# One expert stage: a fixed TensorE order with the side steps in one piece each, and six more weight buffers

## Chip, cores and metric

The kernel runs on one core of one Trainium2 chip. The metric is the time of one execution on the device in microseconds (us), the median of several runs.

## What is computed

The reference is two small transformer blocks in float32, one after the other, on 256 tokens of width 1024. The first has gated linear attention, a dense feed-forward layer, sliding-window attention and a mixture of experts (the stage that this change touches); the second has two layers of differential and forgetting attention on 16 + 256 tokens. The part that matters here:

```python
def moe_swiglu(h, router, w_gate, w_up, w_down):
    t = h.reshape(B * S, D)                          # 256 x 1024
    logits = (t @ router).astype(jnp.float32)        # 8 experts
    top_val, top_idx = lax.top_k(logits, TOP_K)      # 2 of 8
    top_w = jax.nn.softmax(top_val, axis=-1)
    combine = jnp.sum(jax.nn.one_hot(top_idx, N_EXPERTS) * top_w[..., None], axis=1)
    for e in range(N_EXPERTS):
        out = out + combine[:, e:e + 1] * swiglu(t, w_gate[e], w_up[e], w_down[e])
    return out

def swiglu(h, w_gate, w_up, w_down):                 # 1024 -> 2816 -> 1024
    return (jax.nn.silu(h @ w_gate) * (h @ w_up)) @ w_down
```

## The kernel before

**Weights as a stream.** All large weights lie in DRAM in the order of their use, cut into units of 128 x 2048 floats (1024 KB; the gate and up units of an expert's last third are 768 KB). `load` issues one DMA per unit on SP's queue, in the stream's order, each as soon as its buffer is free. In the expert stage the units go round nine buffers: six of the tag `raw` (RING = 6) and three large ones, `rawx` (BIGS = 3). Outside that stage every unit is first split into a high and a low half-precision part (`split_unit`, ScalarE writes `wh`, VectorE `wl`, two pieces of 128 x 1024 each, six buffers of either tag, AHEAD_SPLIT = 6); the experts multiply the raw floats, so these twelve buffers lie idle there.

**The expert stage** (`moe`). A router picks two experts per token; the tokens of an expert are gathered into 96 columns (a "heavy" expert: number 7 and the four fullest of the others) or 64 (a "light" one). An expert has 35 units: per third b of its hidden width eight units of gate and up (`expert_gu`, k = 0 to 7) and four units of down, three in the last third (`expert_down`). `moe_order` lists the 24 thirds of all experts: the gate and up units of one, then the down units of the one before it. A heavy unit is 12 matmuls in the program, a light one 8, on 32 columns of the array each, four side by side; a float32 matmul leaves two records in the trace. The light experts' thirds are strewn between the heavy ones'.

**Side steps.** Between the weight units TensorE also has, per third, the transposes of the hidden values (`hidden`: `eg` and `egb` in, `eh` out by VectorE); per pair of experts to come, four gathers (`chunks`: `G` with `tokH`, then `tokL`) and one step `back` (transposes of `Gb`, and sums with `wrr`); per finished expert, two scatters (`scatter`: `GT` with `yH` and `yL`, into one bank named `mm` for the upper half of the rows and one named `acc` for the lower, which VectorE adds to the residual `h`). `expert_gu` calls `between` after k = 3, which hands out one `hidden`, up to two scatters and up to three gathers. Where each single instruction of them then stands on TensorE is the scheduler's choice by its own estimate of times: only SP's order is written by hand (`manual_schedule` in `run`).

**Into the next stage.** The second block begins with weights that are split again: `split_ahead`, called with every raw unit, splits up to three of them (SPLIT_AHEAD) while the last seven expert units are used. `feed(u)` scales and squares two of the eight 128-row chunks of `h` for the next norm. A branch (`crowded`, L1170), taken only if an expert has too many tokens, stands before the first expert; SP and all others read its count there.

Of the kernel before, what the change touches and what calls it, by code (L numbers as in the profile page):

```python
# [11 lines left out]
F32 = mybir.dt.float32  # L12
# [14 lines left out]
UW = 2048  # L27
# [251 lines left out]
RING = 6  # L279
AHEAD_SPLIT = 6  # L280
BIGS = 3
WORK = 11
AHEAD = RING + BIGS
SPLIT_AHEAD = 3
# [6 lines left out]
class Build:  # L291
# [59 lines left out]
    def load(self, between=None):  # L351
        u = self.next_load
        self.next_load += 1
        i = u - self.moe_range[0] if u in self.moe_range else 0
        if i % (RING + BIGS) >= RING:
            r = self.big("rawx", (128, UW))
        else:
            r = self.ring.tile([128, UW], F32, name="raw", tag="raw", bufs=RING)
        kind, place, rank = self.uses[u]
        w = 4 * int(kind[2:]) if kind[:2] == "gu" else UW  # L360
        n = w // (2 if u < 2 else 1)
        if rank is None:
            src = self.aps["stream"][place]
        else:
            if self.at is None:
                self.at = [self.nc.values_load(self.places[0:1, j:j + 1], engines=[mybir.EngineType.SP],
                                               min_val=EXPERTS_AT, max_val=EXPERTS_AT + 6 * EXPERT_UNITS)
                           for j in range(7)]
            src = self.aps["stream"][bass.ds(self.at[rank] + place, 1)].rearrange("a p w -> (a p) w")
        for i in range(0, w, n):  # L370
            self.nc.sync.dma_start(r[:, i:i + n], src[:, i:i + n])
            if between is not None:
                between(i)
        self.loaded[u] = r

    def raw_unit(self, kind):
        u = self.next_unit
        self.next_unit += 1
        assert self.uses[u][0] == kind, (u, self.uses[u], kind)
        self.split_ahead(u)  # L380
        while u not in self.loaded:
            self.load()
        return self.loaded.pop(u)
# [8 lines left out]

    def split_ahead(self, u):
        n = len(self.halves)
        for v in range(u, min(u + 7, len(self.uses))):
            if v >= u + 1 and not u in self.moe_range:
                break
            if v in self.moe_range or v in self.halves or v < self.split_to:
                continue
            if n >= SPLIT_AHEAD:  # L400
                break
            while v not in self.loaded:
                self.load()
            self.halves[v] = self.split_unit(self.loaded.pop(v), self.uses[v][0])
            self.split_order.append(self.last_high)
            self.split_to, n = v + 1, n + 1

# [566 lines left out]
    def moe(self):  # L974
# [77 lines left out]
        self.prefetch()  # L1052
        self.crowded(cnti)
        late, last, ahead = [], None, []

        starts = dict(zip(HEAVY, GATHERED[1:]))
        for e, kind, b in moe_order():
            units = self.raw_units(e, kind, b)
            if kind == "gu":
# [3 lines left out]

                def between(last=last):
                    if last:
                        st[last] = self.hidden(st[last], last[1])
                    for queue, n in ((late, 2), (ahead, 3)):
                        for f in queue[:n]:
                            queue.remove(f)
                            f()  # L1070

                st[e, b] = self.expert_gu(st[e], b, units, between)
                last = (e, b)
                continue
            if (e, b) == (HEAVY[-1], 2):
                assert not ahead
                st[e, b] = self.hidden(st[e, b], b)
                while late:
                    late.pop(0)()
                self.next_norm("moe")  # L1080
            self.expert_down(st[e], b, st.pop((e, b)), units)
            if b == 2:
                late += self.expert_out(st.pop(e))
        for f in late:
            f()
        for m in range(4):
            self.feed(m)

# [59 lines left out]
    def raw_units(self, e, kind, b):  # L1148

        for u in moe_units(e, kind, b):  # L1150
            r = self.raw_unit(u[0])
            w = chunk(b)[1] if kind == "gu" else 512
            yield [r[:, j * w:(j + 1) * w] for j in range(4)]

# [10 lines left out]
    def crowded(self, cnti):  # L1165
# [4 lines left out]
        with self.tc.If(nc.values_load(cnti[0:1, 0:1], min_val=0, max_val=2 * S) > S, label="crowded"):  # L1170
            p1, pn = (self.t(n, [128, 2, 8], bufs=1) for n in ("pos1", "pos1n"))
            w1, wn = (self.t(n, [128, 2, 8, 2], bufs=1) for n in ("wr1", "wr1n"))
            for r in range(2):
                nc.vector.tensor_sub(p1, self.pos, self.slots[:, None, :].to_broadcast([128, 2, 8]))
                nc.vector.tensor_scalar(p1, p1, -96.0 * r, None, op0=OP.add)
                nc.vector.tensor_copy(w1, self.wr)
                with self.tc.For_i(0, E, 1) as e:
                    X = [self.wk("xg2", (128, 4, 96)) for _ in range(2)]
# [75 lines left out]
    def expert_gu(self, s, b, units, between=None, again=False):  # L1254
# [6 lines left out]
        for k, blk in enumerate(units):  # L1261
# [7 lines left out]
            if not s["light"]:  # L1269
                for j in range(4):  # L1270
                    self.mm1(ps[2][j * GROUP:(j + 1) * GROUP, :W], x[:, 64:96], blk[j], **go)
            if between is not None and k == 3:
                between()
        g = (self.wk if again else self.m2)("eg", [128, 512])
# [10 lines left out]
    def hidden(self, gs, b):  # L1285
# [3 lines left out]
        for g in gs:  # L1289
# [4 lines left out]
            for k in range(n):  # L1294
                self.nc.tensor.transpose(pt[:, k * m:(k + 1) * m], g[:, k * 128:(k + 1) * 128], self.ident[0:m, 0:m])  # L1295
            h = self.wk("eh", (128, 4, m))
            self.nc.vector.tensor_copy(h[:, :n], pt[:, :n * m].rearrange("p (k s) -> p k s", k=n))  # L1297
# [425 lines left out]
```

## Time and profile before

| | |
|---|---|
| median of 3 runs | 1488.23 us (1487.46 to 1488.7) |
| the profiled execution | 1489.77 us |
| its span, first to last instruction | 1488.0 us |
| TensorE busy | 1433.7 us (96%) |
| VectorE, ScalarE busy | 620.2 us, 506.8 us |
| mean granted TensorE clock | 0.985 |
| DMA | 386.90 MB, mean 260 GB/s |

The profile is of one execution. A group of instructions has a busy time, a mean duration and the idle time that stood before it with what ended it. TensorE's records overlap (a matmul begins before the one ahead of it has drained), so the time that a matmul costs is the distance from its start to the next start, not its duration; and a busy TensorE is not yet one at its peak.

### The profile page before, as it was taken

What the parts mean: (1) busy time and instruction counts of PE and PEld (TensorE: products, weight loads), DVE (VectorE), ACT (ScalarE), POOL (GpSimd) and SP (SyncE); (2) the same over time, 40 slices, a digit from 0 to 9 for tenths busy, and PEclk for the clock granted to TensorE, in tenths of its full rate; (3) what the DMA queues carried; (4) which work ended last, traced back from release to release, by engine and by line L of the source; (5) the groups of instructions that cost most, each with busy time, mean ns of one, the idle gap of its engine ahead of it and who ended that gap; (6) DMA issues with size and microseconds to landing.
All of it is one profiled execution on the core that took longest, in us unless ns stands there. A gap on an engine that the chain in (4) does not pass through costs nothing.

```text
span 1488.0 us, 29082 instructions
## 1 busy us (share of the span) xinstructions
PE 1433.7 (96%) x12306; PEld 947.1 (64%) x12306; DVE 620.2 (42%) x1260; ACT 506.8 (34%) x1015; POOL 47.9 (3%) x105
## 2 busy tenths in 40 slices
PE   7999999999979999999999999999998999999997
PEld 7999999998864433333433243333334988898987
DVE  6886555576731011101210020111006876677663
ACT  5766444466411000000100010000005765676563
POOL 1011000010000000000000000000002000010000
PEclk9999999999969999999999999999998999999999
DMA  9433555542408899999989999999998432243300
GB/s 353 163 153 142 192 182 194 189 154 111 175 7 328 321 421 383 381 398 420 419 355 419 421 352 420 419 421 420 419 418 337 142 140 92 92 161 142 114 2 29
DMA packets 58649, 386.90 MB, mean 260 GB/s; under 512 B 7408, under 2 KB 8816, under 8 KB 18448
## 3 DMA queue, kind: packets, MB, share of 16 engines
q1 hardware_dynamic: 58224, 383.64, 65.6%
q8 instruction: 98, 1.61, 0.4%
q0 software_dynamic: 288, 1.34, 0.2%
q14 instruction: 39, 0.32, 0.1%
HBM read 383.90 MB, written 1.05 MB: 259 GB/s over the span
## 4 chain that ended last, share of the span: by engine, by line
PE 62%; DVE 3%; DMA 2%; ACT 2%; issue 1%; DVEq 0%; ACTq 0%
PE mm L436 29%; PE acc L436 16%; PE mm L428 5%; PE mm L429 5%; PE mm L427 5%; DVE wl L433 1%; DMA rawx<-stream 1%; DMA raw<-stream 1%; ACT wh L432 1%; PE acc L1295 1%; PE mm L1295 1%; PE acc L1517 0%; DVE eg L1276 0%; PE acc L1440 0%; DVE h L1342 0%
## 5 line engine op out<-in xcount | busy, mean ns | idle before, releaser
L427 PE MATMUL mm<-xH,wh 128*128 128x256 f32 (+1 forms) x1072 | 309.8, 290 | 13.2 <-ACT wh L432 10.0
L429 PE MATMUL mm<-xH,wl 128*128 128x256 f32 (+1 forms) x1072 | 306.3, 286 | 0.7 <-DVE wl L433 0.7
L428 PE MATMUL mm<-xL,wh 128*128 128x256 f32 (+1 forms) x1072 | 306.2, 286 | 0.7 <-DVE xL L525 0.7
L433 DVE TENSOR_TENSOR wl<-raw,wh 128x1024 fp32r<-128x1024 f32 x198 | 242.0, 1229 | 108.0 <-ACT wh L432 107.7
L432 ACT ACTIVATE wh<-raw 128x1024 fp32r<-128x1024 f32 x198 | 207.2, 1057 | 179.5 <-PE mm L428 118.6
L427 PEld LDWEIGHTS mm<-xH,wh 128*128 128x128 f32 x1072 | 204.0, 191 | 15.9 <-ACT wh L432 10.0
L436 PE MATMUL mm<-raw,xg 128*32 128x512 f32 (+1 forms) x1944 | 209.4, 569 | 4.3 <-DVEq L1170 4.3
L428 PEld LDWEIGHTS mm<-xL,wh 128*128 128x128 f32 x1072 | 203.6, 190 | 2.0 <-DVE xL L525 1.4
L429 PEld LDWEIGHTS mm<-xH,wl 128*128 128x128 f32 x1072 | 203.5, 190 | 1.5 <-DVE wl L433 1.0
L478 ACT ACTIVATE eg<-mm,ws 128x512 f32<-128x512 f32 (+1 forms) x24 | 15.6, 652 | 429.3 <-PE mm L436 429.3
L436 PEld LDWEIGHTS mm<-raw,xg 128*32 128x32 f32 x1944 | 64.0, 111 | 122.2 <-issue 116.5
L436 PE MATMUL acc<-raw,eh 128*32 128x512 f32 x1248 | 141.6, 593 | 0.0
L1276 DVE SCALAR_TENSOR_TENSOR eg<-mm,ws,eg 128x512 f32<-128x512 f32 (+1 forms) x24 | 17.0, 706 | 254.6 <-PE mm L436 254.6
L436 PE MATMUL mm<-rawx,xg 128*32 128x512 f32 (+1 forms) x936 | 97.2, 555 | 0.0
L436 PEld LDWEIGHTS acc<-raw,eh 128*32 128x32 f32 x1248 | 40.1, 110 | 88.0 <-issue 85.9
L436 PE MATMUL mm<-raw,xl 128*32 128x512 f32 (+1 forms) x752 | 80.4, 560 | 0.4 <-DMA raw<-stream 0.4
L427 PE MATMUL mm<-oH,wh 128*128 128x256 f32 (+1 forms) x256 | 73.2, 288 | 0.1
L428 PE MATMUL mm<-oL,wh 128*128 128x256 f32 (+1 forms) x256 | 72.5, 284 | 0.1
L429 PE MATMUL mm<-oH,wl 128*128 128x256 f32 (+1 forms) x256 | 71.9, 281 | 0.0
L436 PE MATMUL acc<-rawx,eh 128*32 128x512 f32 x600 | 69.1, 593 | 0.1
L436 PEld LDWEIGHTS mm<-rawx,xg 128*32 128x32 f32 x936 | 29.8, 110 | 57.5 <-issue 54.6
L1297 DVE COPY eh<-mm 128x512 f32<-128x512 f32 (+3 forms) x19 | 10.2, 538 | 133.9 <-PE mm L1295 133.9
(411 smaller groups left out, 1907.6 us busy)
## 6 DMA issues: line engine op xcount, KB each, us to landing
raw<-stream SPq DMA_DIRECT2D x243, 1024.0 KB, 7.9
rawx<-stream SPq DMA_DIRECT2D x70, 1024.0 KB, 10.8
raw<-stream SPq DMA_DIRECT2D x41, 768.0 KB, 8.5
rawx<-stream SPq DMA_DIRECT2D x23, 768.0 KB, 8.3
raw<-stream SPq DMA_DIRECT2D x4, 512.0 KB, 8.7
h<-xT SPq DMA_DIRECT2D x4, 256.0 KB, 6.5
out<-y SPq DMA_DIRECT2D x4, 256.0 KB, 2.4
pc<-t_gla POOLq DMA_DIRECT2D x1, 384.0 KB, 5.3
```

The costliest lines, as they stand in the source:

```text
L427: mm(out, a[0], b[0], start=start, stop=False, skip_group_check=True)
L428: mm(out, a[0], b[1], start=False, stop=False, skip_group_check=True)
L429: mm(out, a[1], b[0], start=False, stop=stop, skip_group_check=True)
L432: self.last_high = self.nc.scalar.activation(h, src, AF.Copy).ins
L433: self.nc.vector.tensor_sub(l, src, h.bitcast(F32))
L436: self.last_mm = self.nc.tensor.matmul(out, a, b, start=start, stop=stop, skip_group_check=True).ins
L478: self.last_silu = self.nc.scalar.activation(out, src, AF.Silu, **kw).ins
L1276: nc.vector.scalar_tensor_tensor(g[:, :W], ps[1][:, :W], s["rsA"], g[:, :W], op0=OP.mult, op1=OP.mult)
L1295: self.nc.tensor.transpose(pt[:, k * m:(k + 1) * m], g[:, k * 128:(k + 1) * 128], self.ident[0:m, 0:m])
L1297: self.nc.vector.tensor_copy(h[:, :n], pt[:, :n * m].rearrange("p (k s) -> p k s", k=n))
```

## The change

TensorE's order in the expert stage is fixed: `rows_of_experts` is traced under `manual_schedule` for PE, so instructions stand there as the program writes them. `between` is called after every unit: after k = 1 it makes the transposes of the third before, after k = 3 and after k = 5 one whole scatter or gather step. Before the last three down units the scatters now come ahead of the transposes, and two units of the next block are split behind them; `feed` goes 0, 2, 1, 3. Fifteen units instead of nine are loaded ahead: after six `raw` and three `rawx`, six units go as two halves into a `wh` and a `wl` buffer, by two DMAs each; the last fifteen expert units go round the nine as before. The narrow `eh` takes another buffer tag.

```diff
@@ -280,7 +280,8 @@
 AHEAD_SPLIT = 6
 BIGS = 3
 WORK = 11
-AHEAD = RING + BIGS
+EXTRA = 6
+AHEAD = RING + BIGS + EXTRA
 SPLIT_AHEAD = 3
 SCATTER_FROM = 1
 EXPERTS_AT = next(i for i, p in enumerate(stream_plan(ALL)) if p[1].startswith("moe"))
@@ -351,14 +352,19 @@
     def load(self, between=None):
         u = self.next_load
         self.next_load += 1
+
         i = u - self.moe_range[0] if u in self.moe_range else 0
-        if i % (RING + BIGS) >= RING:
+        cycle = AHEAD if i + AHEAD < len(self.moe_range) else RING + BIGS
+        kind, place, rank = self.uses[u]
+        w = 4 * int(kind[2:]) if kind[:2] == "gu" else UW
+        n = w // (2 if u < 2 else 1)
+        if i % cycle >= RING + BIGS:
+            n = w // 2
+            r = [self.ring.tile([128, UW // 2], F32, name=t, tag=t, bufs=AHEAD_SPLIT)[:, :n] for t in ("wh", "wl")]
+        elif i % cycle >= RING:
             r = self.big("rawx", (128, UW))
         else:
             r = self.ring.tile([128, UW], F32, name="raw", tag="raw", bufs=RING)
-        kind, place, rank = self.uses[u]
-        w = 4 * int(kind[2:]) if kind[:2] == "gu" else UW
-        n = w // (2 if u < 2 else 1)
         if rank is None:
             src = self.aps["stream"][place]
         else:
@@ -368,7 +374,7 @@
                            for j in range(7)]
             src = self.aps["stream"][bass.ds(self.at[rank] + place, 1)].rearrange("a p w -> (a p) w")
         for i in range(0, w, n):
-            self.nc.sync.dma_start(r[:, i:i + n], src[:, i:i + n])
+            self.nc.sync.dma_start(r[i // n] if isinstance(r, list) else r[:, i:i + n], src[:, i:i + n])
             if between is not None:
                 between(i)
         self.loaded[u] = r
@@ -377,7 +383,6 @@
         u = self.next_unit
         self.next_unit += 1
         assert self.uses[u][0] == kind, (u, self.uses[u], kind)
-        self.split_ahead(u)
         while u not in self.loaded:
             self.load()
         return self.loaded.pop(u)
@@ -390,20 +395,13 @@
         self.next_unit += 1
         return self.halves.pop(u)
 
-    def split_ahead(self, u):
-        n = len(self.halves)
-        for v in range(u, min(u + 7, len(self.uses))):
-            if v >= u + 1 and not u in self.moe_range:
-                break
-            if v in self.moe_range or v in self.halves or v < self.split_to:
+    def split_ahead(self, u, n=1):
+        for v in range(u, u + n):
+            if v in self.halves:
                 continue
-            if n >= SPLIT_AHEAD:
-                break
             while v not in self.loaded:
                 self.load()
             self.halves[v] = self.split_unit(self.loaded.pop(v), self.uses[v][0])
-            self.split_order.append(self.last_high)
-            self.split_to, n = v + 1, n + 1
 
     def prefetch(self):
         while self.next_load < min(self.next_unit + AHEAD, self.moe_range[-1] + 1):
@@ -1051,7 +1049,15 @@
         steps[-1]()
         self.prefetch()
         self.crowded(cnti)
+        with self.tc.manual_schedule(engines={mybir.EngineType.PE}):
+            self.rows_of_experts(st, gather)
+        for i in (0, 2, 1, 3):
+            self.feed(i)
+
+    def rows_of_experts(self, st, gather):
+
         late, last, ahead = [], None, []
+        self.again = False
 
         starts = dict(zip(HEAVY, GATHERED[1:]))
         for e, kind, b in moe_order():
@@ -1061,30 +1067,29 @@
                     assert not ahead
                     ahead = gather(starts[e])
 
-                def between(last=last):
-                    if last:
+                def between(k, last=last):
+                    if k == 1 and last:
                         st[last] = self.hidden(st[last], last[1])
-                    for queue, n in ((late, 2), (ahead, 3)):
-                        for f in queue[:n]:
-                            queue.remove(f)
-                            f()
+                    elif k in (3, 5) and (late or ahead):
+                        (late or ahead).pop(0)()
 
                 st[e, b] = self.expert_gu(st[e], b, units, between)
                 last = (e, b)
                 continue
-            if (e, b) == (HEAVY[-1], 2):
+            final = (e, b) == (HEAVY[-1], 2)
+            if final:
                 assert not ahead
-                st[e, b] = self.hidden(st[e, b], b)
                 while late:
                     late.pop(0)()
+                st[e, b] = self.hidden(st[e, b], b)
                 self.next_norm("moe")
             self.expert_down(st[e], b, st.pop((e, b)), units)
             if b == 2:
                 late += self.expert_out(st.pop(e))
+            if final:
+                self.split_ahead(self.next_unit, 2)
         for f in late:
             f()
-        for m in range(4):
-            self.feed(m)
 
     def rank_experts(self, sel, cnti):
 
@@ -1150,7 +1155,10 @@
         for u in moe_units(e, kind, b):
             r = self.raw_unit(u[0])
             w = chunk(b)[1] if kind == "gu" else 512
-            yield [r[:, j * w:(j + 1) * w] for j in range(4)]
+            if isinstance(r, list):
+                yield [r[j // 2][:, (j % 2) * w:(j % 2 + 1) * w] for j in range(4)]
+            else:
+                yield [r[:, j * w:(j + 1) * w] for j in range(4)]
 
     def units_again(self, e, kind, b):
 
@@ -1174,6 +1182,7 @@
                 nc.vector.tensor_sub(p1, self.pos, self.slots[:, None, :].to_broadcast([128, 2, 8]))
                 nc.vector.tensor_scalar(p1, p1, -96.0 * r, None, op0=OP.add)
                 nc.vector.tensor_copy(w1, self.wr)
+                self.again = True
                 with self.tc.For_i(0, E, 1) as e:
                     X = [self.wk("xg2", (128, 4, 96)) for _ in range(2)]
                     xs = [[X[c // 2][:, 2 * (c % 2):2 * (c % 2) + 2] for c in range(4)]]
@@ -1269,8 +1278,8 @@
             if not s["light"]:
                 for j in range(4):
                     self.mm1(ps[2][j * GROUP:(j + 1) * GROUP, :W], x[:, 64:96], blk[j], **go)
-            if between is not None and k == 3:
-                between()
+            if between is not None:
+                between(k)
         g = (self.wk if again else self.m2)("eg", [128, 512])
         self.silu(g[:, :W], ps[0][:, :W], scale=s["rsA"])
         nc.vector.scalar_tensor_tensor(g[:, :W], ps[1][:, :W], s["rsA"], g[:, :W], op0=OP.mult, op1=OP.mult)
@@ -1293,7 +1302,7 @@
             pt = self.scratch()
             for k in range(n):
                 self.nc.tensor.transpose(pt[:, k * m:(k + 1) * m], g[:, k * 128:(k + 1) * 128], self.ident[0:m, 0:m])
-            h = self.wk("eh", (128, 4, m))
+            h = (self.wk if m == 128 or self.again else self.m1)("eh", (128, 4, m))
             self.nc.vector.tensor_copy(h[:, :n], pt[:, :n * m].rearrange("p (k s) -> p k s", k=n))
             out.append(h)
         return out
```

TensorE where expert 3 begins (its first gate and up units are `rawx,xg` and `raw,xg`) and expert 7's scatter is due (`GT`). Before:

```order
L436 MATMUL acc<-rawx,eh 32x512 x12
L436 MATMUL acc<-GT,yH 128x256
L436 MATMUL mm<-rawx,xg 32x512 x12
L436 MATMUL mm<-GT,yH 128x256
L436 MATMUL mm<-GT,yL 128x256
L436 MATMUL acc<-GT,yL 128x256
L436 MATMUL mm<-GT,yH 128x256
L436 MATMUL mm<-rawx,xg 32x512 x12
L436 MATMUL acc<-GT,yH 128x256
L436 MATMUL mm<-GT,yL 128x256
L436 MATMUL acc<-GT,yL 128x256
L436 MATMUL mm<-raw,xg 32x512 x12
```

The same place after; the row of transposes (`par,eg`) belongs to the light expert's third before.

```order
L1304 MATMUL acc<-par,eg 128x128 x4
L434 MATMUL mm<-raw,xg 32x512 x24
L434 MATMUL mm<-GT,yH 128x256
L434 MATMUL acc<-GT,yH 128x256
L434 MATMUL mm<-GT,yL 128x256
L434 MATMUL acc<-GT,yL 128x256
L434 MATMUL mm<-GT,yH 128x256
L434 MATMUL acc<-GT,yH 128x256
L434 MATMUL mm<-GT,yL 128x256
L434 MATMUL acc<-GT,yL 128x256
```

The scatter was strewn over single units, with `mm` and `acc` in changing turns; now a whole step of sixteen stands between two units, `mm` and `acc` strictly by turns, and the transposes stand two units into the next third, not at the end of their own.

VectorE before the last three down units, where `eh` is what those units read. Before:

```order
L1326 SCALAR_TENSOR_TENSOR yL<-acc,ws,yH 128x512
L1297 COPY eh<-mm 128x384
L1297 COPY eh<-acc 128x192
L1342 TENSOR_TENSOR h<-h,mm 128x2x256
L1342 TENSOR_TENSOR h<-h,acc 128x2x256
L1342 TENSOR_TENSOR h<-h,mm 128x2x256
L1342 TENSOR_TENSOR h<-h,acc 128x2x256
```

After:

```order
L1335 SCALAR_TENSOR_TENSOR yL<-acc,ws,yH 128x512
L1351 TENSOR_TENSOR h<-h,mm 128x2x256
L1351 TENSOR_TENSOR h<-h,acc 128x2x256
L1351 TENSOR_TENSOR h<-h,mm 128x2x256
L1351 TENSOR_TENSOR h<-h,acc 128x2x256
L1306 COPY eh<-mm 128x384
L1306 COPY eh<-acc 128x192
```

The two copies moved behind the four additions of the last light expert's scatter.

SP, after the loads of the stages before and the first nine expert units (the last rows `raw` and `rawx` here), up to the branch's count:

```order
L377 DMA rawx<-stream 128x2048 x3
L377 DMA wh<-stream 128x1024
L377 DMA wl<-stream 128x1024
L377 DMA wh<-stream 128x1024
L377 DMA wl<-stream 128x1024
L377 DMA wh<-stream 128x1024
L377 DMA wl<-stream 128x1024
```

Twelve loads of 512 KB (six of them shown) came in ahead of SP's read of `cnti`; before, that read followed the three `rawx`.

## Rows read from the trace of the kernel before

**Rows 1.** What SP's queue waited for: us in total, times, longest

```profile
SPq L371 <- PE mm L436: 361.0, 180, 14.3
SPq L371 <- PE acc L436: 152.9, 84, 5.4
```

**Rows 2.** Stretches: length; busy PE, PEld, DVE, ACT, POOL; granted clock, DMA share, GB/s

```profile
439.20:1132.30 693.10, 682.45 (x6393) 244.03 (x6393) 91.13 (x201) 58.63 (x124) 1.65 (x6) 0.99 0.97 393
900.00:920.00 20.00, 20.00 (x191) 6.06 (x183) 0.56 (x1) 0.00 (x0) 0.00 (x0) 1.00 1.01 421
10.00:15.00 5.00, 4.32 (x18) 4.03 (x19) 4.94 (x6) 4.51 (x10) 2.01 (x3) 1.00 1.07 347
862.50:865.00 2.50, 2.50 (x13) 0.61 (x17) 0.36 (x1) 0.33 (x1) 0.00 (x0) 0.50 1.01 420
1135.00:1140.00 5.00, 2.94 (x25) 2.45 (x26) 5.00 (x6) 4.35 (x6) 0.00 (x0) 0.66 0.97 380
```

**Rows 3.** Weight matmuls by group, 439.2 to 1132.4 us: first and last of six

```profile
L436 PE MATMUL mm<-raw,xg 128*32 128x512 f32 (+1 forms) x1944 | 209.4, 569 | 4.3 <-DVEq L1170 4.3
...
L436 PE MATMUL mm<-rawx,xl 128*32 128x512 f32 (+1 forms) x400 | 41.9, 555 | 0.0
```

**Rows 4.** Chain that ended last: start us, us, what

```profile
510.54 0.59 PE acc L1295 x4
511.12 0.39 PE mm L1295 x4
...
590.48 10.30 PE mm L436 x96
...
654.50 15.53 PE mm L436 x192
```

**Rows 5.** TensorE in time, 830 to 870 us: start, us, instruction, [idle before]

```profile
835.06 0.66 PE L1295 MATMUL acc<-par,eg 128*128 128x128 f32 x4 [0.94 <-DVE eg L1276]
...
843.40 2.76 PE L436 MATMUL mm<-rawx,xg 128*32 128x512 f32 x24
...
846.51 2.78 PE L436 MATMUL mm<-rawx,xg 128*32 128x512 f32 x24
...
856.09 0.28 PE L436 MATMUL acc<-GT,yL 64*128 64x256 f32 x1
856.21 0.27 PE L436 MATMUL acc<-GT,yH 64*128 64x256 f32 x1
```

**Rows 6.** TensorE in time, 438 to 470 us: one gather

```profile
454.38 0.68 PE L436 MATMUL mm<-G,tokH 128*128 128x160 f32 x4
...
455.43 5.36 PE L436 MATMUL mm<-raw,xg 128*32 128x512 f32 x48
```

**Rows 7.** TensorE in time, 596 to 606 us: the step `back`

```profile
603.28 0.44 PE L1236 MATMUL acc<-par,Gb 128*128 128x128 f32 x2 [0.35 <-DVE Gb L1206]
...
603.99 1.04 PE L436 MATMUL mm<-raw,xg 128*32 128x512 f32 x2
```

**Rows 8.** TensorE, then VectorE, at the stage's end

```profile
1122.35 0.50 PE L436 MATMUL mm<-GT,yH 64*128 64x256 f32 x2 [0.81 <-ACT yH L1325]
...
1123.36 0.28 PE L436 MATMUL acc<-GT,yL 64*128 64x256 f32 x1
1123.37 0.28 PE L436 MATMUL mm<-GT,yH 64*128 64x256 f32 x1
1123.48 0.28 PE L436 MATMUL acc<-GT,yH 64*128 64x256 f32 x1
...
1124.53 5.36 PE L436 MATMUL acc<-rawx,eh 128*32 128x512 f32 x48
...
1123.80 0.69 DVE L1342 TENSOR_TENSOR h<-h,mm 128x512 f32<-128x512 f32 x1
...
1143.21 5.67 DVE L525 SCALAR_TENSOR_TENSOR xL<-h,g,xH 128x256 fp32r<-128x256 f32 x8
```

**Rows 9.** DMA issues of the page: KB each, median us from issue to landing

```profile
raw<-stream SPq DMA_DIRECT2D x243, 1024.0 KB, 7.9
```

## The prediction, before the changed kernel was run

> **What bounds the kernel now.** I looked first for the engine that the expert stage waits for. The list of SP's waits says it: SP, which issues the weight loads, stood 361.0 + 152.9 = 513.9 us waiting for TensorE to free a buffer [rows 1]. A queue that waits for its consumer is not the bound. The table of stretches agrees: from 439.20 to 1132.30, which is the stage, TensorE is busy 682.45 of 693.10 us [rows 2]. The same row gives the DMA a busy share of 0.97, which would make it look like a second bound; its rate tells more: 393 GB/s over the stage against 421 in a stretch where it is pressed [rows 2], so there is about 7% in hand, not more. A gain on TensorE of much over 7% (some 45 us) would meet the stream.
>
> Busy TensorE is not TensorE at its peak, so the next question is what of the 693 us is weight work. A record costs the distance to the next start. The chain gives this cleanly, since it shows unbroken runs: 96 records in 10.30 us, 107.3 ns each, and in an expert's narrower last third 192 in 15.53 us, 80.9 ns each [rows 4]. A heavy unit leaves 24 records, a light one 16. Five heavy experts of 35 units and three light ones make 5 x 35 x 24 + 3 x 35 x 16 = 5880; the six groups of weight matmuls, 1944 the first and 400 the last, add up to the same [rows 3]. Narrow are the gate and up units of the last thirds, 5 x 8 x 24 + 3 x 8 x 16 = 1344. So 4536 x 107.3 ns + 1344 x 80.9 ns = 486.7 + 108.7 = 595 us. The remaining **98 us** are side steps, the breaks that they make, and waits. Only these can the change move: it touches no weight matmul.
>
> **A strewn step, read in time.** A unit with two pairs of `GT` matmuls strewn into it takes 846.51 - 843.40 = 3.11 us from its start to the next one's [rows 5]; 24 records alone take 24 x 107.3 ns = 2.575. The 0.535 us more are two pairs at 0.12 each (`mm` and `acc` started together, the next 0.12 later: 1123.36, 1123.37, 1123.48 [rows 8]) and about 0.295 for leaving the weight stream and coming back. Two successive `GT` matmuls into the same bank take 0.12 each instead: 856.09, 856.21 [rows 5]. Two of different banks share one slot. Transposes at 835.06 stood 0.94 us because `eg` had just been begun by VectorE [rows 5]; five light thirds of the trace show such a stand.
>
> **The change on TensorE, worked from below.** Each step after the change, priced by rows:
> - Transposes of the hidden values: a full heavy third 0.59 + 0.39 = 0.98 us for two groups of four [rows 4]. Ten of these, five heavy thirds with six transposes (0.74, scaled), six light with four (0.59), three light with three (0.44): 9.8 + 3.7 + 3.5 + 1.3 = 18.3.
> - Gathers: 455.43 - 454.38 = 1.05 us for one [rows 6]; sixteen in the stage: 16.8, as an upper price, for the light pairs are narrower.
> - `back`: 603.99 - 603.28 = 0.71 [rows 7]; eleven such groups in the stage: 7.8.
> - Scatters: all 208 `GT` matmuls now go by turns into `mm` and `acc`, 104 slots where the old order makes 151. Of the 104, 88 lie ahead of the stage's last three units and behind its start: 88 x 0.12 = 10.6.
> - Breaks: the steps stand in 56 pieces between units (68 before): 56 x 0.295 = 16.5.
> - The end: 3 (next paragraph but one). Waits that stay, at the start and at a step whose input is late: 4, an estimate by four stands like the 0.94 above.
>
> Sum: 18.3 + 16.8 + 7.8 + 10.6 + 16.5 + 3 + 4 = **77 us**, against 98. The gain is 21.
>
> **Worked from above,** by what goes: 47 slots of 0.12 = 5.6; twelve breaks = 3.5; five stands at `eg`, which had 0.94 to wait [rows 5] and now have two more units (at least 2 x 16 x 107.3 ns = 3.4 us) between the last gate unit and the transposes, = 4.7. A clock at 0.50 (1.2 GHz, the lower level) in 862.5 to 865 [rows 2], where TensorE did single `GT` matmuls between units, costs half of what runs in it, 1.25 us; if whole steps do not bring it down, that goes too. That makes 15, less 2.7 for the end, 12.3. The remaining 9 us by which the two ways differ would have to be gathers, strewn in chunks whose inputs ScalarE and VectorE were still making; I did not find one row for each. I take a figure near the first way, **20**, since its terms are durations of every step and the second is a list of the losses that I happened to find; 12 is kept as an end of the range.
>
> **The end of the stage.** Now the transposes and the `eh` copies come before the last scatters and the last three down units start at 1124.53 [rows 8]. Afterwards `eh` stands on VectorE behind four additions to `h`. The first began at 1123.80 and took 0.69 [rows 8], so four end at 1126.6 and two copies, taken at 0.3 each by their width against that addition, at 1127.2: 2.7 us later than 1124.53, TensorE idle meanwhile (3 with what the second scatter's wait for `yH`, 0.81 now [rows 8], leaves over). A stand there may also be followed by a lower clock: 0.66 in 1135 to 1140, where TensorE was busy 2.94 of 5 us [rows 2]. The last three units are 72 records, 7.7 us at the upper level and double at the lower, so this end costs 3 to 10.7. I take 3. In return the additions are done sooner, and the splitting of the next block's first two units and `feed` (`xL` starts at 1143.21 [rows 8]) have a shorter way; I cost the tail behind the last unit at 0, from -2 to +2, since the same operations of the same engines stand there in another order.
>
> **The six units ahead.** They do nothing by themselves while SP waits for TensorE. Their twelve DMAs stand on SP ahead of the branch's count, but `wh` and `wl` lie idle by then, so I cost that at nothing; if a buffer were still in use, the stage's start would wait for it, with a unit's 7.9 us from issue to landing [rows 9] as the bound. Their use is that TensorE, being faster, draws the stock down sooner. From the middle of the stage, where gathers give the stream its last long rest (about 846 us after the change), 101 units are left beyond fifteen full buffers, 76 of 1.049 MB and 25 of 0.786, 99.4 MB: at 421 GB/s [rows 2] 236 us, done near 1082. TensorE needs the last near 1106: 24 us in hand. With nine buffers 107 units, 251 us: near 1097, almost bound.
>
> The halves are the unknown. The upper bound is the rate now, 421 GB/s. The lower is the stretch 10 to 15 us, where DMAs of 512 KB and smaller moved 347 [rows 2]. Forty of the 101 units are halves; at 347 each costs 1.049 MB/347 - 1.049 MB/421 = 0.53 us more, 21 us in all, most of the reserve. I take 421, as the stretch of 347 is also the program's first loads with little queued.
>
> The page has loads of 1024 KB that need 7.9 us to land [rows 9] while, at 421 GB/s, one lands each 2.5 us: about three are under way at a time, and the set-up of one is hidden by the others. The Trainium skill, "DMA: Bandwidth & Descriptors", section "Bandwidth", speaks against the halves: it asks for DMAs of at least 1 MiB to reach 75% of the peak, and gives 341 GB/s for a 1-MB transfer issued from GpSimd. Taken as the rate of halves, 341 costs 0.585 us a unit, 23 us, and leaves 1 us of the reserve: the sum stays 1468 by it, and anything below 341, which the rule lets one expect for half the size, would eat the gain. The trace disagrees for whole units, with its 421 GB/s; for halves no stretch of the stage shows it.
>
> **Rivals.**
> Slower, by the stream: halves run so slowly that the DMA sets the end. It decides where a half unit costs more than 1.1 us over a whole one (24 us of reserve and 20 of gain, over forty units), which is 1.049 MB in 3.59 us, 292 GB/s. At 280 GB/s it costs 1.26 more, 50 us less the 44, so 1494. For it: a DMA share of 0.97 leaves little. Against it: 347 is the worst row with small loads.
> Slower, by the fixed order: TensorE now stands at every step whose input is late, and the weight work behind it cannot go ahead, as it could when the scheduler chose. Over 56 pieces 0.38 us each cancels 21 us; with the 0.94 of the light thirds at half of them the kernel stands at 1468 + 26 = 1494. Against it: each step is called two units, 3.4 to 5.2 us, after the one that feeds it, and VectorE and ScalarE are busy 91 and 59 of 693 us [rows 2].
> Little: the list from above is the whole gain, 12, and the end takes up to 7.7 of it more: 4 to 12 are left, 1476 to 1484. For it: I found no rows for the other 9. Against it: the sum from below has a row for each kind of step.
> Better: the end costs nothing and the lower clock goes everywhere, 1456 to 1460.
>
> **How the numbers follow.** The profiled execution took 1489.77 us against the median of 1488.23; all sums are differences, and I take them off the median: 1488.2 - 20 = **1468**. A measurement tells about 0.2% (3 us) from no change. Chances: the forecast, gains of 14 to 26, 0.62; little, 3 to 14, 0.18; better 0.08; no change that can be told 0.05; the stream 0.03; the fixed order 0.04. The range is the forecast with most of the little and some of the better, 1460 to 1479. Faster 0.88, same 0.05, slower 0.07.
>
> **What would show it.** Weight records at the same 107.3 and 80.9 ns; `GT` starts in couples all through the stage; no transposes waiting for `eg`; the stage near 673 us and its last three units behind a stand of about 3 us after the scatters; SP still waiting for TensorE, though for less than 514 us, and no unit of TensorE waiting for a landing; wide stretches at 421 GB/s also where halves go. The prediction is wrong if the halves lower that rate, if TensorE has stands at `yH`, `G` or `eh` in most of its 56 pieces, or if a break costs more than 0.295 us when the step is long.

## The result, and the profile after

The changed kernel takes 1467.88 us (median of 4 runs, 1467.61 to 1468.13) against 1488.38 before: 0.9863 of it, 95% interval 0.9846 to 0.9880. The forecast was 1468. Its profiled execution has a span of 1466.4 us, 21.6 less than before. The gain is all in the expert stage: from the first expert matmul to the last the trace of before has 1131.98 - 439.23 = 692.75 us, the one of after 1110.61 - 438.70 = 671.91, 20.8 less; behind the stage 356.0 and 355.8 us are left.

That the number came out does not yet mean that every term did. First SP's waits, after (as [rows 1]: us in total, times, longest):

```profile
SPq L377 <- PE mm L434: 133.2, 107, 14.2
SPq L377 <- DMA raw<-stream: 129.1, 70, 7.1
...
SPq L377 <- DMA rawx<-stream: 77.2, 42, 3.2
...
SPq L377 <- DMA wh<-stream: 52.5, 75, 0.9
SPq L377 <- PE acc L434: 52.2, 39, 9.5
SPq L377 <- DMA wl<-stream: 50.6, 73, 2.3
```

SP waits 185 us for TensorE where it was 514 [rows 1], and 309 us for transfers of its own queue to land, where it was 29 (25.4 for `raw`, 3.6 for `rawx`). The loads have become a bound beside TensorE; I had expected SP to go on waiting for TensorE. The stretches of after (columns as in [rows 2]) say the same:

```profile
438.70:1110.90 672.20, 664.91 (x6393) 233.86 (x6393) 93.95 (x203) 60.49 (x126) 1.64 (x6) 0.99 0.99 398
900.00:920.00 20.00, 20.00 (x211) 7.43 (x210) 4.93 (x14) 4.39 (x13) 0.00 (x0) 1.00 1.02 413
```

The rate in the pressed stretch is 413 GB/s, not the 421 of [rows 2]. TensorE near the stage's end, after (start, us, instruction, idle before):

```profile
1056.48 1.50 PE L434 MATMUL mm<-raw,xl 128*32 128x384 f32 x16 [0.39 <-DMA raw<-stream]
1058.35 1.50 PE L434 MATMUL mm<-raw,xl 128*32 128x384 f32 x16 [0.37 <-DMA raw<-stream]
1060.23 1.50 PE L434 MATMUL mm<-rawx,xl 128*32 128x384 f32 x16 [0.38 <-DMA rawx<-stream]
```

One narrow light unit each 1.88 us, where its 16 records take 16 x 80.9 ns = 1.29: TensorE works as fast as units land. Over eight units between 1046 and 1095 us such waits come to 5.8 us.

What went as forecast: a scatter is one piece, with its records in couples at 0.12 us,

```profile
561.08 0.38 PE L434 MATMUL mm<-GT,yH 64*128 64x256 f32 x1
561.08 0.38 PE L434 MATMUL acc<-GT,yH 64*128 64x256 f32 x1
561.30 0.28 PE L434 MATMUL mm<-GT,yL 64*128 64x256 f32 x1
561.30 0.28 PE L434 MATMUL acc<-GT,yL 64*128 64x256 f32 x1
561.41 0.28 PE L434 MATMUL mm<-GT,yH 64*128 64x256 f32 x1
...
562.22 1.07 PE L434 MATMUL mm<-raw,xg 128*32 128x512 f32 x8
```

and the transposes wait for `eg` no more. Their group in the stage, before and then after (busy, mean ns, idle before and what ended it):

```profile
L1295 PE MATMUL acc<-par,eg 128*128 128x128 f32 x48 | 8.3, 288 | 5.3 <-DVE eg L1276 5.1
```

```profile
L1304 PE MATMUL acc<-par,eg 128*128 128x128 f32 x41 | 6.9, 287 | 0.0
```

The end of the stage, after, TensorE and then VectorE:

```profile
1099.80 0.40 PE L1304 MATMUL acc<-par,egb 64*128 64x64 f32 x3 [0.43 <-DVE h L1351]
1101.47 7.05 PE L434 MATMUL acc<-rawx,eh 128*32 128x512 f32 x48 [1.26 <-DVE eh L1306]
...
1100.26 0.68 DVE L1351 TENSOR_TENSOR h<-h,acc 128x512 f32<-128x512 f32 x1
1100.86 0.55 DVE L1306 COPY eh<-mm 128x384 f32<-128x384 f32 x1
```

The copy of `eh` stands behind the four additions, as worked out, and TensorE behind the copy. Its 48 records then take 7.05 us, not the 5.36 of [rows 8], at a granted clock of 0.50, that is 1.2 GHz (columns as in [rows 2]):

```profile
1102.00:1105.00 3.00, 3.00 (x20) 0.76 (x16) 0.00 (x0) 0.69 (x1) 0.00 (x0) 0.50 1.01 421
```

Ahead of it stood 5.5 us of which TensorE was idle some 3. That is the end's other price: 1.7 us, of the 7.7 that it could have been.

### The profile page after: what moved, and what is told of

The parts are those of the page before. It is cut to its first block, busy times and chain, and to the rows that moved or that the text cites. A ratio compares the mean times of both kernels' runs of the same rounds, so it can differ in the third digit from the quotient of the medians.

```text
span 1466.4 us, 29487 instructions
## 1 busy us (share of the span) xinstructions
PE 1415.7 (97%) x12306; PEld 935.8 (64%) x12306; DVE 621.2 (42%) x1260; ACT 506.4 (35%) x1015; POOL 48.5 (3%) x105
## 3 DMA queue, kind: packets, MB, share of 16 engines
HBM read 383.90 MB, written 1.05 MB: 263 GB/s over the span
## 4 chain that ended last, share of the span: by engine, by line
PE 62%; DVE 3%; DMA 3%; ACT 2%; issue 1%; DVEq 0%; ACTq 0%; SPq 0%
PE mm L434 29%; PE acc L434 16%; PE mm L426 5%; PE mm L425 5%; PE mm L427 5%; DMA rawx<-stream 2%; DVE wl L431 1%; ACT wh L430 1%; DMA wl<-stream 1%; PE mm L1304 1%; PE acc L1304 1%; PE acc L1526 0%; ACT rt L1439 0%; DVE xL L523 0%; PE acc L1449 0%
## 5 line engine op out<-in xcount | busy, mean ns | idle before, releaser
L434 PE MATMUL mm<-raw,xg 128*32 128x512 f32 (+1 forms) x1200 | 124.7, 563 | 4.3 <-DVEq L1178 4.3
L434 PE MATMUL acc<-raw,eh 128*32 128x512 f32 x848 | 94.2, 592 | 0.5 <-DMA raw<-stream 0.5
L434 PEld LDWEIGHTS mm<-raw,xg 128*32 128x32 f32 x1200 | 38.5, 111 | 79.5 <-issue 76.4
L434 PE MATMUL mm<-wh,xg 128*32 128x512 f32 (+1 forms) x540 | 87.0, 576 | 0.0
L434 PE MATMUL mm<-wl,xg 128*32 128x512 f32 (+1 forms) x540 | 82.1, 573 | 0.0
L434 PEld LDWEIGHTS acc<-raw,eh 128*32 128x32 f32 x848 | 27.6, 110 | 63.8 <-issue 60.0
L1306 DVE COPY eh<-mm 128x512 f32<-128x512 f32 (+3 forms) x19 | 10.7, 562 | 121.1 <-PE mm L1304 121.1
L434 PE MATMUL mm<-rawx,xg 128*32 128x384 f32 (+1 forms) x600 | 58.4, 534 | 0.0
L1306 DVE COPY eh<-acc 128x512 f32<-128x512 f32 (+3 forms) x20 | 10.7, 537 | 94.6 <-PE acc L1304 94.6
```

The source lines that it names most:

```text
L434: self.last_mm = self.nc.tensor.matmul(out, a, b, start=start, stop=stop, skip_group_check=True).ins
```

## The experiments

All ratios are to the kernel before, run on the same chip.

**The parts of the change.** First the six units alone, put into the kernel before:

```diff
-AHEAD = RING + BIGS
+EXTRA = 6
+AHEAD = RING + BIGS + EXTRA
```
(with `load` and `raw_units` as in the change)

> The kernel before with nothing but the six more units ahead in halves. Theory: there TensorE was slow enough for nine buffers, so the units bring at most the few us that its last light thirds waited for landings: 1484 to 1488. Rival (the buffers are a main part of the gain): 1475 to 1482. Rival (halves hurt): 1490 or more.

1484.90 us, 0.9971 (0.9962 to 0.9981): 3.7 us less, within the theory's range but not by the theory's reason. TensorE in the kernel before waits only 0.6 us for landings in the whole stage. The scheduler, which still chooses the order here, chose another one: 53 units of the stage have side steps in them, where it was 64, and the units with steps are 86.3 us too long, where it was 91.7. What the six units are worth under the old order itself this run does not tell, beyond those 0.6 us. Then the order without the units:

```diff
-EXTRA = 6
+EXTRA = 0
```

> The changed kernel with its order on TensorE, but nine units ahead as before (no units in the halves). Theory: after the change the weight stream is a second bound beside TensorE; the six units are 6.2 MB of stock at the stage's start (15 us at 413 GB/s) and are paid for by a rate of 413 instead of 420 GB/s (about 11 us over 260 MB). So 3 to 6 us slower than the changed kernel: 1471 to 1474. Rival of the prediction (nine buffers are almost enough, the stream has slack): 1466 to 1469. Rival (the stock is all that counts): 1479 to 1483.

1474.83 us, 0.9906 (0.9891 to 0.9921): 7 us slower than the change, a little past the theory's upper end and past the prediction's "almost bound". TensorE's waits for landings rise from about 6 to 11 us (17 units, from the 230th on), although the stream flows faster; stretches of e1 and of the change:

```profile
800.00:900.00 100.00, 100.00 (x953) 35.65 (x946) 13.18 (x31) 6.75 (x13) 0.00 (x0) 1.00 1.01 420
```

```profile
800.00:900.00 100.00, 100.00 (x955) 36.09 (x947) 13.19 (x31) 6.91 (x14) 0.00 (x0) 1.00 1.02 413
```

420 GB/s with whole units alone, 413 with forty in a hundred as halves. Each against its own measurement of the kernel before, the units alone gain 3.7 us (most of it by another order), the new order alone 13.3, and both 20.5. The waits for landings, 0.6 us before, 11 with the new order and nine buffers and 5.8 with fifteen, say that only the faster order needs the stock.

**Fixed order or places?** The same places for the steps, the order left to the scheduler:

```diff
-        with self.tc.manual_schedule(engines={mybir.EngineType.PE}):
-            self.rows_of_experts(st, gather)
+        self.rows_of_experts(st, gather)
```

> The changed kernel without the order by hand: the same calls of between at k = 1, 3 and 5 and the same fifteen units ahead, but the scheduler chooses TensorE's order in the stage. Theory (the fixed order is what keeps a step in one piece): steps are strewn again, with single GT matmuls between units and steps put where their input is just made: 1474 to 1484. Rival (the places at which the program calls the steps are enough): 1466 to 1470.

1478.19 us, 0.9928 (0.9911 to 0.9944). Up to expert 3 its pieces are nearly those of the change (each `back` is cut in two); from expert 4 on they are strewn: steps lengthen 90 units of the stage, where it is 56 in the change, by 84 us against 66 (both counted as the distance to the next unit's start less the records at their 107.3 or 80.9 ns). Waits for `eg` are back, 3.0 us in all:

```profile
L1303 PE MATMUL acc<-par,eg 128*128 128x128 f32 x41 | 7.1, 288 | 3.0 <-DVE eg L1284 2.9
```

Now the fixed order with all steps of a third at the old place, k = 3:

```diff
-                    if k == 1 and last:
-                        st[last] = self.hidden(st[last], last[1])
-                    elif k in (3, 5) and (late or ahead):
-                        (late or ahead).pop(0)()
+                    if k == 3:
+                        if last:
+                            st[last] = self.hidden(st[last], last[1])
+                        for queue, n in ((late, 2), (ahead, 3)):
+                            for f in queue[:n]:
+                                queue.remove(f)
+                                f()
```

> The changed kernel, order fixed by hand, but between hands out at k = 3 all that it handed out before: a third's transposes, two scatter and three gather steps one behind the other. Theory (the small steps at places of their own are what a fixed order needs): TensorE stands at gathers and scatters whose buffers and inputs ScalarE and VectorE have not done, some 1 us at each of the twelve places with several steps: 1472 to 1482. Rival (the fixed order and fewer breaks are all; fewer breaks even help): 1462 to 1468.

1482.97 us, 0.9967 (0.9955 to 0.9979): most of the gain is gone, with the order as fixed as in the change. A step stands behind the one ahead of it. TensorE in one such piece, between two scatters and before the gathers:

```profile
562.84 0.28 PE L434 MATMUL mm<-GT,yL 64*128 64x256 f32 x1
563.90 0.39 PE L434 MATMUL mm<-GT,yH 64*128 64x256 f32 x1 [0.78 <-DVE h L1354]
...
565.90 0.68 PE L434 MATMUL mm<-G,tokH 128*128 128x160 f32 x4 [0.78 <-DVE h L1354]
```

Each waits 0.78 us for a bank that VectorE is still adding to `h`. This is the rival "slower, by the fixed order" at work, and it shows what keeps it away in the change: the steps' distance. There is a second loss. At the end of some long pieces, or right behind them, the granted clock falls, here behind one that ended at 601.95 (hidden, gather and `back`, 5 us without a weight unit):

```profile
603.00:605.00 2.00, 2.00 (x13) 0.42 (x8) 0.00 (x0) 0.00 (x0) 0.00 (x0) 0.50 1.02 408
```

There are five such stretches in the stage, of 3 to 7 us, and the weight unit behind each of these pieces is 1.5 to 1.7 us too long. The kernel before has one, from 860 to 867 us, which begins among the three gathers that stand directly behind most of two scatter steps in one unit, not at single `GT` matmuls as I had read [rows 2]; it cost up to 3.5 us, where I had priced the 2.5 us of [rows 2] at 1.25. In the change the clock is at 0.50 only at the stage's start (as before) and at its end.

**The price of a scatter.** The same sixteen matmuls of a step, per half of the bank first four into `mm` and then four into `acc`:

```diff
-            for j, (y, GT) in enumerate(terms):
-                for c in range(2):
+            for c in range(2):
+                for j, (y, GT) in enumerate(terms):
```

> The changed kernel with the GT matmuls of a scatter first all into mm and then all into acc, instead of by turns. Prediction's price: a slot of 0.12 us is shared by two, so 80 slots more ahead of the last down units: 9.6 us on TensorE, 12 in all with the steps of the end. If TensorE alone is the bound: 1478 to 1480. Theory of two bounds: about 6 us of that take the place of waits for landings: 1472 to 1475. Rival (turns bring nothing): 1467 to 1469.

1467.71 us, 0.9864 (0.9849 to 0.9879): no change. The trace says why; a step in time:

```profile
559.66 0.28 PE L434 MATMUL mm<-GT,yH 64*128 64x256 f32 x1
559.67 0.28 PE L434 MATMUL acc<-GT,yH 64*128 64x256 f32 x1
559.78 0.28 PE L434 MATMUL mm<-GT,yL 64*128 64x256 f32 x1
559.79 0.28 PE L434 MATMUL acc<-GT,yL 64*128 64x256 f32 x1
```

They still start in couples, though the program writes four of one bank first. The two halves of the array's rows (`mm` takes rows 0 to 63, `acc` 64 to 127) go on side by side, written by turns or four and four, if both have work in the queue. My price "by turns, 104 slots for 151" had the right sum by the wrong reason. The Trainium skill, "TensorE: Matmul & The Clock Gate", section "Part 3: Packing small matmuls — row/col tiling", states a part of this: the engine pulls a weight load for a row group that does not conflict ahead of matmuls in flight, within a window of 64. It also has the matmuls themselves start in the program's order, and there this trace differs: the `acc` matmul at 559.67 starts ahead of the `mm` one at 559.78, which the program has before it. If the halves need work at the same time, a step must lose when one half's matmuls stand far from the other's. I tried it on the kernel e7 below, where the loads are no bound: eight `GT` matmuls into `mm` at one place, the eight into `acc` at the next (k = 3 to 6):

```diff
-        return [lambda m=m: self.scatter(s, m, ys) for m in range(2)]
+        return [lambda m=m, c=c: self.scatter(s, m, ys, c) for m in range(2) for c in range(2)]
```
(with `scatter` and `between` changed to match)

> The kernel with one buffer for wh and wl and the hidden values ahead of the last scatters, in which each scatter step is cut in two pieces at places of their own (k = 3 to 6): first the eight GT matmuls into mm, a unit later the eight into acc. Theory (the two halves of the array work side by side only if both have GT matmuls at hand, in whatever order; apart, each slot of 0.12 us holds one): ten steps more pieces at some 0.25 us and eighty slots more, 2.5 + 9.6: 1468 to 1472 against 1458. Rival (a slot is not shared, turns and halves are of no account): only the breaks, 1460 to 1462.

1472.48 us against 1458.24, 0.9893 (0.9876 to 0.9909): 14.2 more, just past the theory's upper end. The scatter pieces of the stage take 26.65 us where they took 13.14, with 24 of them for 12. A half step is eight slots at 0.12, one matmul in each:

```profile
560.53 0.28 PE L433 MATMUL mm<-GT,yH 64*128 64x256 f32 x1
560.65 0.28 PE L433 MATMUL mm<-GT,yL 64*128 64x256 f32 x1
...
561.33 2.78 PE L433 MATMUL mm<-raw,xg 128*32 128x512 f32 x24
```

Each half of the rows has a bank of its own here, so these runs do not tell whether it is the rows or the banks that let two matmuls share a slot.

**The halves.** Every expert unit by two DMAs, the whole buffers too:

```diff
-        n = w // (2 if u < 2 else 1)
+        n = w // (2 if u < 2 or u in self.moe_range else 1)
```

> The changed kernel with every expert unit loaded by two DMAs of half its size (512 or 384 KB), the whole buffers too. Theory (halves cost rate, 1.7% for 40% of the units): rate near 403 GB/s instead of 413, some 14 us more of a stream that is a bound: 1478 to 1484. Rival (halves cost nothing): 1467 to 1469.

1475.38 us, 0.9909 (0.9894 to 0.9924): 7.5 slower than the change, half of what I had expected, at 405 GB/s, near the 403 expected:

```profile
800.00:900.00 100.00, 100.00 (x955) 36.10 (x943) 13.19 (x31) 6.99 (x15) 0.00 (x0) 1.00 1.03 405
```

And the opposite, `wh` and `wl` as two halves of one buffer, so that the six units come by one DMA each:

```diff
-            n = w // 2
-            r = [self.ring.tile([128, UW // 2], F32, name=t, tag=t, bufs=AHEAD_SPLIT)[:, :n] for t in ("wh", "wl")]
+            r = self.ring.tile([128, UW], F32, name="whl", tag="whl", bufs=AHEAD_SPLIT)
...
-            h = self.ring.tile([128, n], F32R, name="wh", tag="wh", bufs=AHEAD_SPLIT)
-            l = self.ring.tile([128, n], F32R, name="wl", tag="wl", bufs=AHEAD_SPLIT)
+            hl = self.ring.tile([128, 2 * n], F32R, name="whl", tag="whl", bufs=AHEAD_SPLIT)
+            h, l = hl[:, :n], hl[:, n:]
```

> The changed kernel with wh and wl as two halves of one buffer of 128 x 2048, so that the six extra units are loaded by one DMA of 1024 KB each (2 x 6 buffers of 512 KB become 6 of 1024 KB; a half of wh and of wl then come free together in the other stages). Theory: the halves cost the 1.7% of rate (413 against 420 GB/s), and about 6 us of TensorE's waits for landings near the stage's end go: 1460 to 1463, with the stretches of the stage at 419 to 422 GB/s. Rival (the rate fell because the stream is pressed all the time, not by the halves): 411 to 415 GB/s and 1466 to 1469.

1462.38 us, 0.9825 (0.9812 to 0.9838), 5.5 faster than the change, at the rate of whole units:

```profile
800.00:900.00 100.00, 100.00 (x954) 36.15 (x947) 13.37 (x32) 7.46 (x17) 0.00 (x0) 1.00 1.01 419
```

Of TensorE's 6 us of waits for landings 0.4 are left. So no halves, forty in a hundred, all: 420, 413, 405 GB/s. It is the halves that cost the rate.

**The end.** The transposes and `eh` ahead of the last scatters again:

```diff
-                while late:
-                    late.pop(0)()
                 st[e, b] = self.hidden(st[e, b], b)
+                while late:
+                    late.pop(0)()
```

> The changed kernel with the transposes and copies of the hidden values ahead of the last scatters again, as before. Theory: the last three down units start some 2.3 us earlier and meet no lower clock (1.7 us): 1464 to 1466. Rival (the tail behind the stage, with its splits and feed, takes it back): 1467 to 1468.5.

1462.95 us, 0.9830 (0.9816 to 0.9843): 4.9 faster than the change, more than expected. The place before the last three down units takes 3.13 us, not 5.52, and the units behind it run at the upper clock: 2.4 + 1.7 = 4.1. The lower clock is not gone, though: it has moved behind the stage (1104.98 here).

```profile
1097.00:1105.00 8.00, 8.00 (x84) 2.64 (x80) 3.61 (x5) 1.38 (x2) 0.13 (x1) 1.00 1.02 420
1114.10:1117.40 3.30, 3.30 (x16) 3.19 (x15) 3.30 (x4) 3.30 (x11) 3.30 (x4) 0.50 0.70 295
```

Behind the stage the clock is at 0.50 for 6.8 us, where it is 3.4 in the change, and this part takes 357.8 us for 355.8. So in the profiled run the stage gains 5.2 us and the tail takes 2.0 of it back, which is the rival in part. In the profiled runs of e7 and e10, which end the same way, the tail is 357.9 and 356.8 us. This run took 1464.80 us, 1.9 more than its median; whether the tail is as long in the other four the record does not show.

**Both together.**

> Both: one buffer for wh and wl, so that all units come by one DMA, and the hidden values ahead of the last scatters. Theory: the gains add up, 6 and 3: 1457 to 1461. Rival (the stream or the tail takes one of them back): 1462 to 1466.

1458.24 us, 0.9800 (0.9786 to 0.9813), the fastest: 9.6 less than the change, where the two single gains are 5.5 and 4.9. Its stage, and its end:

```profile
438.50:1100.50 662.00, 661.49 (x6393) 233.66 (x6393) 92.76 (x202) 59.74 (x125) 1.65 (x6) 1.00 0.99 402
```

```profile
1090.67 0.38 PE L433 MATMUL mm<-GT,yH 64*128 64x256 f32 x1
...
1092.75 5.36 PE L433 MATMUL acc<-rawx,eh 128*32 128x512 f32 x48
```

TensorE is idle for 0.5 us of 662 and waits for no landing. SP waits 362 us for TensorE and 162 for landings: TensorE is the bound again, with the stream close behind.

## Why the prediction was right, and where its steps were not

The sum was 77 us beside the weight work, and the trace of after has 671.9 - 595.4 = 76.5. Its terms stand like this (a piece is measured as above, the breaks are in it):

| | predicted, us | measured, us |
|---|---|---|
| transposes of the hidden values, 23 places ahead of the end | 24.3 | 20.6 |
| gathers, 16 | 21.5 | 18.5 |
| `back` | 9.0 | 8.1 |
| scatters ahead of the end, 12 units | 13.1 | 13.2 |
| the end: `eh` late, transposes, two scatter steps of eight | 5.0 | 5.5, and 1.7 at the lower clock |
| start and waits | 4 | 2.2 (the lower clock at the start, as before), and 5.8 for landings |
| sum | 77 | 75.6, and 0.9 over the rest |

(The predicted column is each row's work with 0.295 us for each of its breaks; at the end eight slots of 0.12, the transposes at 0.74, a break and 3.)

- **What bounds the kernel, and the weight work:** right. The records kept their 107.3 and 80.9 ns; all that moved was beside them.
- **Breaks:** counted twice in part. The times of the transposes, of a gather and of `back` [rows 4, 6, 7] were taken up to the next weight matmul, so they already contained the way back into the weights: a whole gather costs 1.13 to 1.17 us with its break, not 1.05 + 0.295. The terms of transposes, gathers and `back` were 7.6 us too large. The scatters, whose price was made of slots, came out to 0.1.
- **Scatters:** right sum, wrong reason. That couples need turns fell with e5; that both halves need work at the same time was shown by e10.
- **The six units and the stream:** the step that failed. I took fifteen full buffers at 846 us for granted. In the trace of after the stream is pressed from about 500 us on, and at 835 us a unit is used 11.5 us after it has landed, not 36 us as at 509 us, when the fifteen buffers were still full; the 24 us in hand were nothing. The rate of 421 became 413, which over the 101 units is 4.6 us more. It is why the six units are worth 7 us with the new order (e1), and why some 6 us of waits for landings appeared that stood in no term. They made up for most of the breaks that I had counted twice: that 1468 was met to 0.1 us is luck, the gain of some 20 us is not.
- **The end:** the mechanism was right, and the size within the 3 to 10.7 us that I had given: 5.5 us for the 5.0 worked out, and 1.7 us of lower clock behind them. Before, the scatters at this place took 3.2 us and the transposes, a few units earlier, 1.3; so 4.5 us became 7.2, 2.8 more. With the two in the other order (e3) it is 3.1. The tail at 0 was right (356.0 and 355.8 us).
- **The list from above** had 15 us of gains, less 2.7 for the end. The steps ahead of the end cost 87.2 us before and 60.4 after, and 2.2 us of lower clock in the weight unit behind one of them are gone too: 29 us, of which 2.8 at the end and 5.2 more of waits for landings were lost again. So the list had half of what was gained. If each record of a step before is priced as after (13.2/160 us for a `GT` record, 20.6/137 for a transpose, 18.5/128 for a gather's), the rest shows: transposes at places of their own took 26.1 us where they would take 16.1, and I had 4.7 for the stands at `eg`; three units with three gathers and scatters one behind the other are 21.3 us too long, where it would be 15.9; and the clock's stretch was 7 us long, not 2.5. That waits stand between steps so close together, e8 shows. Some 4 us of smaller places stay without a row.
- **The rivals:** the fixed order's waits are real, with the lower clock behind them 15 us in e8, and kept away by the places; the stream did become a bound, but took about 6 us, not 20 or more. Two units are 2.6 us in a narrow light third, not 3.4 at the least, but no stand came of it. "Little" and "better" did not come true.
- **The Trainium skill's rule** of at least 1 MiB per DMA ("DMA: Bandwidth & Descriptors", section "Bandwidth") points the right way here, 420 against 405 GB/s; its 341 GB/s for a 1-MB transfer is not what these streams show.

Not tested: why the lower clock comes with some long pieces and not with others (in e8 the ones that end at 569 and 711, of 8 to 9 us, have none, and one of 4 us at 940 has it); the price of a break by itself; and the small parts of the change by themselves (two units split instead of up to three, the order of `feed`, the other tag of the narrow `eh`).

## What to carry to other kernels

When an order is fixed by hand, the places count as much as the order: a step must stand far enough behind the one that feeds it or shares its banks, or the engine stands there with everything queued behind it (1468 against 1483 us here). Price a side step from the start of the last weight unit ahead of it to the start of the next one, once, so that no break is counted twice. When the bounding engine is made faster, work out the stock of the next stream from its first full buffer on, not from a point in the middle, and look whether the last steps put a wait in front of work that is ready.

## What the runs showed that I had not expected

- Loads of 512 KB instead of 1024 KB cost 1.7% of the rate for forty units in a hundred and 3.6% for all (420, 413, 405 GB/s), with several of them under way. Once the stream is a bound this is 5.5 us.
- TensorE's two halves of rows run `GT` matmuls side by side even if the program writes four of one half and then four of the other; apart from each other a step of sixteen costs twice its slots.
- Ahead of the stage's end e8 has seven pieces of 4 to 9 us without weight units. With five of them TensorE's clock was granted at 0.50 for 3 to 7 us; behind the change's pieces of 0.6 to 2.3 us there it stayed at 1.00.
